# Hybrid decoder layer: the gated recurrence in two lanes of two heads, with half-width score products for the long levels

## The chip, the cores and the metric

The kernel runs on one core of a Trainium2 chip. The metric is the device time of one execution in microseconds (us); before the change the median of three runs is 2064.65 us (2059.46 to 2064.86).

## The reference

The input is a sequence of 1024 tokens of width 1024; 16 learned meta tokens go in front. One layer is computed: a half-weighted SwiGLU feed-forward network, a mixer, and a second half-weighted SwiGLU network, each behind an RMS norm. The mixer projects its input once and runs two groups of heads side by side. The change concerns the four heads of the gated recurrence (HGRN2), which works on blocks of 128 tokens:

```python
bcum = cumsum(logf)                     # per block of 128 tokens, per key channel
o_inter = (q * exp(bcum)) @ S           # what came from earlier blocks
attn[t, s] = sum_d q[t,d] * k[s,d] * exp(bcum[t,d] - bcum[s,d])   for s <= t
o = o_inter + attn @ v
S = exp(b_last)[:, None] * S + (k * exp(b_last - bcum)).T @ v
```

Each head's output is RMS-normed and gated. The other group is stick-breaking attention. Then `h = h + concat(o_recurrence, o_stickbreaking) @ w_out`.

## The kernel before

The layer is a chain of stages: first feed-forward network, projection, attention of the stick-breaking heads (with the projections of the recurrence filled in between), the recurrence, the output product, second feed-forward network. TensorE's instructions run in the order in which the program writes them; those of the other engines are placed by the tile scheduler. Every engine works its own queue in order.

**The recurrence** (`hgrn_attend`, one generator per head, each `yield` one piece of work). A head holds queries `QA`, keys `KB` and gates `F` with the 128 key channels on the partitions and the tokens along the row, and values `vT`. The decay inside a block of 128 tokens is built up in levels of n = 1, 2, 4, 8, 16, 32 and 64 tokens. At level n, blocks of 2n tokens are halved: queries of the later half meet keys of the earlier half. `level` (L870) makes the whole 128 x 128 products of all queries and all keys for the eight blocks of a head (tile `lvl`, L855, eight products, in two PSUM banks of four), and takes out of them only the pairs that belong to this level: for n up to 8 VectorE copies under a mask (L886), from n = 16 on ScalarE copies rectangles (L877). Then VectorE multiplies the later queries by the gate product of the earlier half (L904), the earlier keys by that of the later half (L908), and forms the next level's gate products `Ts` (L914). So the next level's score products wait for this level's two multiplications, which wait for this level's products. One product in float32 is two passes of TensorE, which the trace counts as two instructions. Ahead of the levels comes a diagonal (L864); behind them the keys are transposed (`km`, `knp`, L920 to L928), the block states `S` are made (`s`, `up`, L934 to L944), the output is formed (`op`, L954 and L957), normed (L962 to L967), transposed back (`onp`, L973) and split into high and low part for the output product (`oH`, L975 to L981).

**The fill.** Half of the output product, that of the stick-breaking heads, does not need the recurrence. It is 64 steps of three products with 512 columns (`wo<-...oT`, L1267), in groups of four steps for each of 16 tiles; each group reads a tile `oT` from memory, ends in an addition on VectorE (`res`, L1663) and a store (`hmN`). Its weights come from `w_out` (`mix_weights`, `split_w`): a load into `raw` (L140, two buffers), a cast into a high half `wh` on ScalarE (L145), a difference `wl` on VectorE (L147). Sixteen such weight tiles are loaded while the recurrence runs: eight for the fill, eight for the second half of the output product (`wo<-...oH`), which starts when all heads are done.

**The order.** `weave` (L1306) takes turns between the lanes and the fill by a clock: each piece yields an estimate of its TensorE time and a delay until its lane may go on. A lane that may go on comes first. The fill is held back while its spent share is ahead of the lanes' done work (`total`, `work`). Before the change there are three lanes: heads 0 and 3 one after the other, head 1, head 2. The tiles of a head exist three times; head 3 takes over the buffers of head 0. PSUM has eight banks here: two for the fill, two `z` for scores, two `tr` for transposes and states, two `o` for outputs.

Of the kernel before, what the change touches and what calls it, by code (L numbers as in the profile page):

```python
# [11 lines left out]
F32 = mybir.dt.float32  # L12
# [8 lines left out]
P = 128  # L21
# [3 lines left out]
META = 16  # L25
# [14 lines left out]
class Block:  # L40
# [784 lines left out]
    def hgrn_attend(self, h, pool, src, oH):  # L825
        nc = self.nc
# [8 lines left out]
        at8 = tile_of("attn", SEQ).rearrange("p (c t) -> p c t", t=P)  # L835
# [5 lines left out]
        ss, sq = tile_of("ss", 8), tile_of("sq", P)  # L841
        yield 0, 4000

        ps = self.flip(vT, [(0, META)])
        nc.vector.tensor_copy(vm, ps[:META, 0, :])
        for q in range(2):
            ps = self.flip(vT, [(META + (4 * q + j) * P, P) for j in range(4)])
            nc.scalar.copy(vr[:, 4 * q : 4 * q + 4, :], ps)
# [16 lines left out]

        def later(x, n):

            return x.rearrange("p (b h r) -> p b h r", h=2, r=n)[:, :, 1, :]

        def level(i, n):  # L870
            nb = P // (2 * n)
            m = later(self.masks[:, i, :], n).unsqueeze(1).broadcast_to([P, 4, nb, n])
            for half in range(2):
                ps = scores(half)
                if n >= 16:
                    for s in range(0, P, 2 * n):
                        nc.scalar.copy(  # L877
                            attn[half][s : s + n, :, s + n : s + 2 * n],
                            ps[s : s + n, :, s + n : s + 2 * n],
                        )  # L880
                    continue
                out, src = (
                    x.rearrange("p c (b h r) -> p c b h r", h=2, r=n)[:, :, :, 1, :]
                    for x in (attn[half], ps)
                )
                nc.vector.copy_predicated(out, m, src)  # L886

        diagonal()
        nc.vector.tensor_mul(QA, QA, F[:, META:])
# [1 line left out]
        tn = F  # L891
        at = 0
        for i, n in enumerate(LEVELS):
            level(i, n)
            if n <= 8:
                kb = KB.rearrange("p (b h r) -> p b h r", h=2, r=n)
                tk = tn[:, : T // n].rearrange("p (b h) -> p b h", h=2)
            else:
                kb = KB[:, META:].rearrange("p (b h r) -> p b h r", h=2, r=n)
                tk = tn[:, 1 : 1 + SEQ // n].rearrange("p (b h) -> p b h", h=2)  # L900
            nb = kb.shape[1]
            qa = QA.rearrange("p (b h r) -> p b h r", h=2, r=n)
            nq = qa.shape[1]
            nc.vector.tensor_mul(  # L904
                qa[:, :, 1, :], qa[:, :, 1, :],
                tk[:, nb - nq :, 0:1].broadcast_to([P, nq, n]),
            )
            nc.vector.tensor_mul(  # L908
                kb[:, :, 0, :], kb[:, :, 0, :], tk[:, :, 1:2].broadcast_to([P, nb, n])
            )  # L910
            o = 0 if n <= 8 else 1
            nt = Ts[:, at : at + nb + o]
            at += nb + o
            nc.vector.tensor_mul(nt[:, o : o + nb], tk[:, :, 0], tk[:, :, 1])  # L914
            tn = nt
            yield 1740, 2600
        dec = tn

        km = self.ptr.tile([P, P], F32, tag="tr", name="km")
        nc.tensor.transpose(km[:META, :], KB[:, :META], self.ident)  # L920
        nc.vector.tensor_copy(kms, km[:META, :])
        kn = vT[:, :SEQ].rearrange("p (c d) -> p c d", d=P)
# [7 lines left out]
        nc.sync.dma_start(g, src["g"][h])  # L930
        yield 960, 2000
        S = F[:, :SEQ].rearrange("p (c d) -> p c d", d=P)
        ps = self.ptr.tile([P, P], F32, tag="tr", name="s0")
        nc.tensor.matmul(ps, kms, vm, start=True, stop=True)  # L934
        nc.vector.tensor_copy(S[:, 0, :], ps)
        for q in range(2):
            ps = self.ptr.tile([P, 4, P], F32, tag="tr", name="up")
            js = [j for j in range(4) if 4 * q + j < 7]
# [413 lines left out]
    def run(self):  # L1352
# [20 lines left out]
        with ExitStack() as c0:  # L1373
# [258 lines left out]
            with tc.manual_schedule(engines={nc.tensor.engine}):  # L1632
                right, cx, pre = ExitStack(), ExitStack(), ExitStack()
                with ExitStack() as c1:
# [41 lines left out]
                    with ExitStack() as c2:  # L1676
# [3 lines left out]
                        self.pz = self.pool("pz2", 2, PSUM, c2)  # L1680
                        self.ptr = self.pool("ptr2", 2, PSUM, c2)
                        self.po = self.pool("po2", 2, PSUM, c2)
                        lanes = [chain(heads[0], heads[3]), heads[1], heads[2]]
                        self.weave(first_half_of_o(), lanes, 64 * 680.0 + 5000.0, 4 * 21900.0)

                    def begin(i, b):
                        if b not in h:
# [165 lines left out]
```

## Time and profile before

| | us |
|---|---|
| profiled execution, its time | 2062.77 |
| its span in the trace | 2061.0 |
| median of three runs | 2064.65 |
| first recurrence product to first `oH` product | 1212.67 to 1368.40 |

The span's 1.77 us less than the time lies around the program. In the table of groups each row has a line, engine, operation and tile, the count, the busy time and mean of one, and the idle time before it with what ended it. Timeline rows begin with the start in us and the duration; rows of the same kind that follow closely are merged, with their count behind `x`. A TensorE row's duration has the pipeline's end in it, so the cost of a row in a dense stretch is read from the start of one to the start of the next.

### The profile page before, as it was taken

To read this page: it belongs to the slowest core of one execution; us is meant where nothing else is said; L and a number is where in the kernel's file an instruction comes from. 1 tells how busy PE (TensorE), PEld (TensorE's weight loads), DVE (VectorE), ACT (ScalarE), POOL (GpSimd) and SP (SyncE) were. 2 spreads that over 40 slices of the span, in tenths; PEclk is the share of its full clock that TensorE was granted. 3 is DMA by queue.
4 is the path that set the end of the run, shared out by engine and by line. 5 is a ranking of instruction groups with operands and counts; after the bars stand their busy time and mean duration, and the time that the engine had idled before them with its cause. 6 is when DMAs were issued, how large, how long until landed. Compare 5 with 4: busy or idle time off the path is not lost.

```text
span 2061.0 us, 31571 instructions
## 1 busy us (share of the span) xinstructions
PE 2004.8 (97%) x11249; PEld 1782.3 (86%) x11249; DVE 1376.6 (67%) x2069; ACT 901.2 (44%) x1855; POOL 638.6 (31%) x696
## 2 busy tenths in 40 slices
PE   7999999999999999999999999999999999999999
PEld 7999999999987899988887878888888888878887
DVE  6867745556688842257878757648677677666774
ACT  7633332334554534456666623336333333234443
POOL 2366644542000002243443300210564454441000
PEclk9999999999999999999999999999999999999999
DMA  8643322227875645435454262684343333349573
GB/s 237 192 145 113 112 79 94 99 76 232 285 219 171 226 135 169 147 123 130 116 144 114 64 223 88 195 272 137 112 131 105 95 110 102 97 150 346 185 229 113
DMA packets 289647, 314.96 MB, mean 153 GB/s; under 512 B 24080, under 2 KB 218000, under 8 KB 289488
## 3 DMA queue, kind: packets, MB, share of 16 engines
q1 hardware_dynamic: 272304, 260.83, 41.1%
q0 software_dynamic: 16144, 52.10, 6.6%
q8 instruction: 89, 1.46, 0.3%
q14 instruction: 70, 0.57, 0.1%
q10 hardware_dynamic: 1040, 0.00, 0.0%
HBM read 228.62 MB, written 84.23 MB: 152 GB/s over the span
## 4 chain that ended last, share of the span: by engine, by line
PE 83%; DVE 7%; DMA 3%; ACT 3%; issue 2%; POOL 0%; SPq 0%; DVEq 0%; POOLq 0%; ACTq 0%
PE o L599 16%; PE qb L313 15%; PE qa L313 10%; PE qc L313 10%; PE proj L162 5%; PE proj L160 5%; PE proj L161 5%; PE qd L313 4%; PE o L561 3%; PE wo L1267 3%; PE flip L1086 2%; DVE wl L270 1%; PE lvl L855 1%; DVE keep L1232 1%; PE oacc L1156 1%
## 5 line engine op out<-in xcount | busy, mean ns | idle before, releaser
L313 PE MATMUL qb<-T,wh 128*128 128x384 f32 (+1 forms) x1056 | 317.8, 362 | 0.0
L270 DVE TENSOR_TENSOR wl<-s,wh 128x512 fp32r<-128x512 f32 x176 | 198.8, 1130 | 95.2 <-ACT wh L268 91.1
L313 PEld LDWEIGHTS qb<-T,wh 128*128 128x128 f32 x1056 | 195.8, 188 | 21.5
L313 PE MATMUL qa<-B,wh 128*128 128x384 f32 (+1 forms) x704 | 213.9, 367 | 0.3 <-ACT sg L415 0.3
L599 PE MATMUL o<-wl,th 128*128 128x512 f32 x539 | 209.9, 391 | 3.7 <-DVE wl L520 3.7
L599 PE MATMUL o<-wh,tl 128*128 128x512 f32 x539 | 209.6, 390 | 0.7 <-DVE tl L520 0.7
L599 PE MATMUL o<-wh,th 128*128 128x512 f32 x539 | 209.9, 391 | 0.0
L268 ACT CAST wh<-s 128x512 fp32r<-128x512 f32 x176 | 109.4, 621 | 223.2 <-PE qb L313 164.1
L160 PE MATMUL proj<-xh,wh 128*128 128x384 f32 (+2 forms) x576 | 205.0, 356 | 0.2 <-ACT xh L250 0.2
L270 DVE TENSOR_TENSOR wl<-raw,wh 128x512 fp32r<-128x512 f32 x184 | 170.1, 926 | 52.2 <-ACT wh L268 48.7
L161 PE MATMUL proj<-xh,wl 128*128 128x384 f32 (+2 forms) x576 | 199.1, 346 | 0.0
L162 PE MATMUL proj<-xl,wh 128*128 128x384 f32 (+2 forms) x576 | 198.9, 345 | 0.1
L268 ACT CAST wh<-raw 128x512 fp32r<-128x512 f32 x184 | 113.6, 620 | 184.1 <-PE qc L313 100.4
L313 PE MATMUL qb<-T,wl 128*128 128x384 f32 (+1 forms) x528 | 192.0, 364 | 0.9 <-DVE wl L270 0.9
L518 ACT CAST th<-act 128x512 fp32r<-128x512 f32 (+2 forms) x176 | 96.6, 550 | 178.1 <-PE o L599 120.0
L520 DVE TENSOR_TENSOR tl<-act,th 128x512 fp32r<-128x512 f32 (+2 forms) x176 | 105.5, 602 | 64.9 <-ACT th L518 63.7
L313 PE MATMUL qd<-X,wh 128*128 128x272 f32 x704 | 144.4, 292 | 2.0 <-DVE sp L397 1.6
L283 POOL TENSOR_TENSOR s<-raw 128x512 f32<-128x512 f32 x88 | 122.6, 1393 | 74.8 <-DVE wl L270 60.1
L313 PEld LDWEIGHTS qa<-B,wh 128*128 128x128 f32 x704 | 130.5, 188 | 16.5 <-ACT sg L415 0.7
L1232 DVE TENSOR_TENSOR_SCAN keep<-keep 128x144 f32<-128x144 f32 (+6 forms) x112 | 127.1, 1138 | 8.3 <-ACT keep L1228 6.0
L1237 POOL TENSOR_TENSOR sig<-sig,keep 128x144 f32<-128x144 f32 (+3 forms) x64 | 88.2, 1378 | 141.7 <-DVE keep L1232 75.6
L313 PE MATMUL qa<-B,wl 128*128 128x384 f32 (+1 forms) x352 | 128.8, 366 | 0.8 <-DVE wl L270 0.8
(343 smaller groups left out, 4761.1 us busy)
## 6 DMA issues: line engine op xcount, KB each, us to landing
raw<-in_ffn_w_in_dram SPq DMA_DIRECT2D x228, 256.0 KB, 3.0
raw<-in_ffn_w_out_dram SPq DMA_DIRECT2D x176, 256.0 KB, 4.3
raw<-in_w_in_dram SPq DMA_DIRECT2D x28, 512.0 KB, 4.5
ks<-kD SPq DMA_DIRECT2D x32, 260.0 KB, 5.6
oT<-oD SPq DMA_DIRECT2D x32, 256.0 KB, 4.7
ak<-in_ffn_w_out_dram SPq DMA_DIRECT2D x22, 256.0 KB, 5.3
v<-vD SPq DMA_DIRECT2D x8, 576.0 KB, 4.8
vD<-vhl SPq DMA_DIRECT2D x8, 512.0 KB, 3.9
```

Of the source, the lines that this page charges most:

```text
L160: nc.tensor.matmul(ps, wh[:, s], xs, start=k == 0, stop=False)
L161: nc.tensor.matmul(ps, wl[:, s], xs, start=False, stop=False)
L162: nc.tensor.matmul(ps, wh[:, s], xl[:, k, c0 : c0 + n], start=False, stop=k == nk - 1)
L268: nc.scalar.copy(hi, src)
L270: nc.vector.tensor_sub(lo, src, hi.bitcast(F32))
L283: op(t, x, y)
L313: nc.tensor.matmul(ps, a[:, k, :], b[:, k0 + k, :], start=start and k == 0 and i == 0, stop=k == 3 and i == 2, skip_group_check=True,)
L518: nc.scalar.copy(hi, src)
L520: nc.vector.tensor_sub(lo, src, hi.bitcast(F32))
L599: nc.tensor.matmul(banks[bank][m], z[:, m * P : (m + 1) * P], y, start=start and q == 0 and e == 0, stop=q == nq - 1 and e == 2, skip_grou ...
L1232: nc.vector.tensor_tensor_scan(out=kv, data0=kv, data1=kv, initial=1.0 if last else keep[:, end : end + 1], op0=ALU.mult, op1=ALU.bypass,)
L1237: nc.gpsimd.tensor_mul(sig, sig, keep[:, 1 : nk + 1])
```

## The change

Six edits, all in the recurrence and its weaving:

1. Levels of n = 4 and more multiply only the later halves of the queries: the moving operand has 64 columns in place of 128, read as runs of n with gaps of n. The keys stay whole as the stationary operand. All eight blocks of a head fit in one bank, so a level holds one bank in place of two. Levels 1 and 2 and the diagonal stay as they were.
2. The copies out of PSUM for these levels cover all eight blocks at once: one masked copy of 128 x 512 in place of two of 128 x 256 (n = 4, 8), and half as many rectangles, twice as long (n = 16, 32, 64).
3. `level` returns its copies, and they are issued behind the two multiplications of the level in place of ahead of them.
4. The transposed meta values (`vmp`), the keys' meta rows (`km`) and the first state (`s0`) take a bank of `o` in place of `tr`; two small copies go from VectorE to ScalarE.
5. The yield of a level of n = 4 and more says 960 ns in place of 1740.
6. Two lanes, heads 0 and 2 and heads 1 and 3, in place of three; the work estimate for the fill's share is 4 * 18000 in place of 4 * 21900.

```diff
-        ps = self.flip(vT, [(0, META)])
-        nc.vector.tensor_copy(vm, ps[:META, 0, :])
+        ps = self.po.tile([P, P], F32, tag="o", name="vmp")
+        nc.tensor.transpose(ps[:META, :], vT[:, :META], self.ident)
+        nc.scalar.copy(vm, ps[:META, :])
...
         def level(i, n):
...
-            for half in range(2):
-                ps = scores(half)
-                if n >= 16:
-                    for s in range(0, P, 2 * n):
-                        nc.scalar.copy(
-                            attn[half][s : s + n, :, s + n : s + 2 * n],
-                            ps[s : s + n, :, s + n : s + 2 * n],
-                        )
-                    continue
...
+            if n < 4:
+                m = m.unsqueeze(1).broadcast_to([P, 4, nb, n])
+                return [
+                    (later(attn[half], n), m, later(scores(half), n)) for half in range(2)
+                ]
+            ps = self.pz.tile([P, 8, P // 2], F32, tag="z", name="lvl")
+            for c in range(8):
+                nc.tensor.matmul(
+                    ps[:, c, :].rearrange("p (b r) -> p b r", r=n),
+                    KB[:, META + c * P : META + (c + 1) * P],
+                    later(QA[:, c * P : (c + 1) * P], n), start=True, stop=True,
+                )
+            if n < 16:
+                m = m.unsqueeze(1).broadcast_to([P, 8, nb, n])
+                return [(later(at8, n), m, ps.rearrange("p c (b r) -> p c b r", r=n))]
+            return [
+                (at8[s : s + n, :, s + n : s + 2 * n], None, ps[s : s + n, :, s // 2 : s // 2 + n])
+                for s in range(0, P, 2 * n)
+            ]
...
-            level(i, n)
+            copies = level(i, n)
...
+            for out, m, got in copies:
+                if m is None:
+                    nc.scalar.copy(out, got)
+                else:
+                    nc.vector.copy_predicated(out, m, got)
...
-            yield 1740, 2600
+            yield 960 if n >= 4 else 1740, 2600
...
-        km = self.ptr.tile([P, P], F32, tag="tr", name="km")
+        km = self.po.tile([P, P], F32, tag="o", name="km")
...
-        ps = self.ptr.tile([P, P], F32, tag="tr", name="s0")
+        ps = self.po.tile([P, P], F32, tag="o", name="s0")
         nc.tensor.matmul(ps, kms, vm, start=True, stop=True)
-        nc.vector.tensor_copy(S[:, 0, :], ps)
+        nc.scalar.copy(S[:, 0, :], ps)
...
-                        lanes = [chain(heads[0], heads[3]), heads[1], heads[2]]
-                        self.weave(first_half_of_o(), lanes, 64 * 680.0 + 5000.0, 4 * 21900.0)
+                        lanes = [chain(heads[0], heads[2]), chain(heads[1], heads[3])]
+                        self.weave(first_half_of_o(), lanes, 64 * 680.0 + 5000.0, 4 * 18000.0)
```

The number of TensorE passes is the same on both sides. Where they stand is not. On TensorE at the start of the recurrence (`flip`: transposes of the values, 128x64: the half-width products), before:

```order
L855 MATMUL lvl<-QA,KB 128x128 x16
L1086 MATMUL flip<-ident,vT 16x128
L1086 MATMUL flip<-ident,vT 128x128 x8
L855 MATMUL lvl<-QA,KB 128x128 x168
L920 MATMUL km<-ident,KB 16x128
```

and now:

```order
L856 MATMUL lvl<-QA,KB 128x128 x32
L1281 MATMUL wo<-wh,oT 128x512
L1281 MATMUL wo<-wl,oT 128x512
L1281 MATMUL wo<-wh,oT 128x512 x2
L1281 MATMUL wo<-wl,oT 128x512
L1281 MATMUL wo<-wh,oT 128x512
L856 MATMUL lvl<-QA,KB 128x128 x16
L1281 MATMUL wo<-wh,oT 128x512
```

Before, three heads went through nearly all levels with no fill between; now two do, and six fill products stand between the levels 1 and 2, six more behind level 2, and then by turns three and six between the half-width products of one head and the other. The second pair of heads is woven with nine fill products at a time.

On VectorE at the same place (`wl`: the low halves of the fill's weights, `Ts`: gate products; `128x128x2` is the masked copy of level 2), where the first weight half stood behind the work of several levels before:

```order
L914 TENSOR_TENSOR Ts<-Ts 128x130
L914 TENSOR_TENSOR Ts<-Ts 128x32
L147 TENSOR_TENSOR wl<-raw,wh 128x512
L904 TENSOR_TENSOR QA<-QA,Ts 128x32x16
L908 TENSOR_TENSOR KB<-KB,Ts 128x32x16
```

and now:

```order
L147 TENSOR_TENSOR wl<-raw,wh 128x512
L928 TENSOR_TENSOR Ts<-Ts 128x32
L928 TENSOR_TENSOR Ts<-Ts 128x16
L147 TENSOR_TENSOR wl<-raw,wh 128x512
L928 TENSOR_TENSOR Ts<-Ts 128x8
L147 TENSOR_TENSOR wl<-raw,wh 128x512 x2
L924 COPY_PREDICATED attn<-masks,lvl 128x128x2
L913 TENSOR_TENSOR QA<-QA,Ts 128x256x2
```

The first weight half stood at level 16 (`128x32x16` is its multiplication) and now stands ahead of the copies of level 2, with all four halves of the fill's first column block in a row.

At the end of the recurrence on TensorE, before, the last head's output products and transposes:

```order
L957 MATMUL op<-vr,attn 128x128
L1267 MATMUL wo<-wh,oT 128x512
L1267 MATMUL wo<-wl,oT 128x512
L1267 MATMUL wo<-wh,oT 128x512 x2
L1267 MATMUL wo<-wl,oT 128x512
L1267 MATMUL wo<-wh,oT 128x512 x2
```

and now:

```order
L968 MATMUL op<-F,QA 128x128
L971 MATMUL op<-vr,attn 128x128
L987 MATMUL onp<-ident,vT 128x128 x8
L1281 MATMUL wo<-wh,oH_13950 128x512
L1281 MATMUL wo<-wl,oH_13950 128x512
```

Fifteen fill products stood behind the last `op` and nine behind the last `onp`; now no fill is left there, and the last transposes follow the last output products directly.

More of the change, by code (lines that the diff above doesn't have):

```diff
@@ L866, in later @@
         def later(x, n):
+            if len(x.shape) == 3:
+                return x.rearrange("p c (b h r) -> p c b h r", h=2, r=n)[:, :, :, 1, :]
             return x.rearrange("p (b h r) -> p b h r", h=2, r=n)[:, :, 1, :]
@@ L871, in level @@
             nb = P // (2 * n)
-            m = later(self.masks[:, i, :], n).unsqueeze(1).broadcast_to([P, 4, nb, n])
-            for half in range(2):
-                ps = scores(half)
-                if n >= 16:
-                    for s in range(0, P, 2 * n):
-                        nc.scalar.copy(
-                            attn[half][s : s + n, :, s + n : s + 2 * n],
-                            ps[s : s + n, :, s + n : s + 2 * n],
-                        )
-                    continue
-                out, src = (
-                    x.rearrange("p c (b h r) -> p c b h r", h=2, r=n)[:, :, :, 1, :]
-                    for x in (attn[half], ps)
-                )
-                nc.vector.copy_predicated(out, m, src)
+            m = later(self.masks[:, i, :], n)
+            if n < 4:
[9 more added lines that the diff above has]
+                    later(QA[:, c * P : (c + 1) * P], n), start=True, stop=True,
+                )
+            if n < 16:
[5 more added lines that the diff above has]
+            ]
         diagonal()
```

## The prediction

> **What bounds the kernel now.** I read the head of the page, then the busy time by stage of the recurrence and what follows it, then the groups in it, then its timeline.
>
> ```profile
> PE 2004.8 (97%) x11249; PEld 1782.3 (86%) x11249; DVE 1376.6 (67%) x2069; ACT 901.2 (44%) x1855; POOL 638.6 (31%) x696
> ```
> ```profile
> core 0: us, PE busy (x) PEld busy (x) DVE busy (x) ACT busy (x) POOL busy (x), PEclk, DMA share, GB/s
> 1212.60:1270.00 57.40, 51.70 (x416) 47.10 (x413) 52.09 (x104) 19.46 (x58) 0.00 (x0) 1.00 0.42 141
> 1270.00:1368.40 98.40, 92.10 (x588) 80.09 (x587) 56.75 (x115) 31.36 (x111) 16.84 (x22) 1.00 0.67 213
> 1368.40:1418.50 50.10, 49.47 (x242) 41.08 (x242) 32.61 (x49) 22.99 (x47) 7.08 (x10) 1.00 0.57 195
> ```
>
> TensorE is busy for 97% of the whole, so a gain must come from less TensorE work or from fewer gaps in it. The first of the three stretches is the levels of three heads without fill: VectorE is busy 52.09 of 57.40 us there and is as near its limit as TensorE. In the second, the fill is woven in and VectorE has slack (56.75 of 98.40). The third is the second half of the output product; it starts when all heads are done, and the change does not touch it. So the prediction is about one number: when that half starts. Before, the recurrence runs from 1212.67 to 1368.40, that is 155.7 us.
>
> ```profile
> 1212.67 1.70 PE L1086 MATMUL flip<-ident,vT 128*16 128x128 f32 x10
> ```
> ```profile
> L1267 PEld LDWEIGHTS wo<-wh,oH x128: 186/188/190, 1368.4 to 1418.1; 128*128 128x128 f32 x128
> ```
>
> How much of it is TensorE work? The groups give the counts, dense stretches of the timeline the prices.
>
> ```profile
> L855 PE MATMUL lvl<-QA,KB 128*128 128x128 f32 x512 | 63.7, 279 | 4.3 <-DVE attn L886 2.5 <-ACT attn L877 1.3 <-DVE attn L864 0.2
> L1267 PE MATMUL wo<-wh,oT 128*128 128x512 f32 x128 | 44.6, 407 | 1.0 <-DMA oT<-oD 1.0
> L1267 PE MATMUL wo<-wl,oT 128*128 128x512 f32 x64 | 25.2, 394 | 0.0
> L954 PE MATMUL op<-F,QA 128*128 128x128 f32 x64 | 12.4, 276 | 0.8 <-ACT sq L962 0.8
> L957 PE MATMUL op<-vr,attn 128*128 128x128 f32 x64 | 12.4, 275 | 0.0
> L941 PE MATMUL up<-vr,vT 128*128 128x128 f32 x56 | 7.6, 284 | 0.5 <-DVE F L935 0.4
> L1086 PE MATMUL flip<-ident,vT 128*128 128x128 f32 (+1 forms) x36 | 5.4, 279 | 2.1 <-DVE vm L845 1.1 <-ACT vr L848 0.9
> L927 PE MATMUL knp<-ident,KB 128*128 128x128 f32 x32 | 4.8, 281 | 1.6 <-ACT vT L928 1.2 <-DVE kms L921 0.4
> L973 PE MATMUL onp<-ident,vT 128*128 128x128 f32 x32 | 4.2, 273 | 0.0
> ```
> ```profile
> 1303.04 0.39 PE L954 MATMUL op<-F,QA 128*128 128x128 f32 x2
> ...
> 1304.83 1.95 PE L855 MATMUL lvl<-QA,KB 128*128 128x128 f32 x16
> ...
> 1308.02 1.08 PE L973 MATMUL onp<-ident,vT 128*128 128x128 f32 x8
> 1308.85 0.48 PE L1267 MATMUL wo<-wh,oT 128*128 128x512 f32 x1
> ...
> 1324.05 1.95 PE L855 MATMUL lvl<-QA,KB 128*128 128x128 f32 x16
> 1325.75 0.48 PE L1267 MATMUL wo<-wh,oT 128*128 128x512 f32 x1
> 1326.06 0.39 PE L1267 MATMUL wo<-wl,oT 128*128 128x512 f32 x1
> ...
> 1328.63 0.49 PE L855 MATMUL lvl<-QA,KB 128*128 128x128 f32 x3
> ```
>
> From start to start: 16 score passes take 1325.75 - 1324.05 = 1.70 us, .106 each; twelve fill products 2.88, .24 each (the first costs .31, .08 more than the later .23); the 16 passes of `op` 1.79, .112 each; eight transposes .83, .104 each. Work: 512 x .106 = 54.4, 192 x .24 = 46.1, 128 x .112 = 14.3, 56 x .112 = 6.3, 100 x .104 = 10.4, sum 131.5 us. The other 24.2 us are waits (with a few small passes, on both sides alike). Until the first fill product at 1270, 368 score passes and 45 transposes were done, 43.7 us of work in 57.3: 13.6 us of waits there, 10.6 in the rest.
>
> **The change, part by part.**
>
> *Half-width products.* 20 groups of 16 passes (five levels, four heads) move 64 columns in place of 128. What such a pass costs, no row shows directly. The nearest is the small product of the first norm, also float32 with 128 columns of weights, which moves one column:
>
> ```profile
> L173 PE MATMUL nps<-ones_d,nacc x6: 163/214/250, 570.0 to 570.4; 128*128 128x1 f32 x4, 128*16 128x1 f32 x2
> ```
> ```profile
> 569.96 0.19 PEld L173 LDWEIGHTS nps<-ones_d,nacc 128*128 128x128 f32 x1
> ...
> 570.07 0.19 PEld L173 LDWEIGHTS nps<-ones_d,nacc 128*128 128x128 f32 x1
> ...
> 570.18 0.19 PEld L173 LDWEIGHTS nps<-ones_d,nacc 128*128 128x128 f32 x1
> ```
>
> The first row gives the shape, the others the start of three weight loads in a row. They follow each other at .11 us, as the score passes do, though almost nothing is moved. So a float32 pass with fresh weights of 128 columns costs .11 whatever it moves, and the keys are still loaded whole. I take no gain: 320 x 0. The other end is a pass in which the moved columns set the pace; the nearest row is the attention's output, of another number format, 128 columns in .06:
>
> ```profile
> 1198.36 0.23 PE L1156 MATMUL oacc<-wu,v 128*128 128x128 f32 x1
> 1198.42 0.22 PE L1158 MATMUL oacc<-wu,v 128*64 128x128 f32 x1
> ```
>
> By that, 320 x (.106 - .055) = 16.3 us of work would go. Above zero: the columns are now read with gaps, which no row shows; I hold a loss for unlikely, since the moved columns would have to cost twice what they do. The Trainium skill ("TensorE: Matmul & The Clock Gate", Back-to-back issue gap) gives the gap of a lone matmul by the columns moved, 134 cycles for 128 and about 60 for 64, by which the passes would halve; the same page (LDWEIGHTS) sets the load by the weight's columns, P / 1.2 ns, 107 ns for 128. The first rule would give the sum with 16.3 us off, the second the sum with nothing off, and the .11 us of the row with one moved column agree with the second.
>
> *More turns between scores and fill.* The fill stands in 30 groups in place of 18; 12 x .08 = 1.0 us.
>
> *Copies.* On VectorE 16 masked copies of 256 become 8 of 512.
>
> ```profile
> L886 DVE COPY_PREDICATED attn<-masks,lvl 128x256 f32<-128x256 uint8 x32 | 17.7, 577 | 4.4 <-PE lvl L855 4.0
> L904 DVE TENSOR_TENSOR QA<-QA,Ts 128x512 f32<-128x512 f32 x24 | 16.6, 691 | 4.2 <-PE lvl L855 4.2
> L908 DVE TENSOR_TENSOR KB<-KB,Ts 128x520 f32<-128x520 f32 (+1 forms) x24 | 16.4, 685 | 0.0
> ```
>
> One of 512 costs between .58 and 1.15. A level of two heads at n = 4 and 8 then needs 2 x (.69 + .69) + 2 x (.58 to 1.15) = 3.9 to 5.1 us of VectorE, against 2 x 1.70 + 9 x .24 = 5.6 us of TensorE: covered. The copies leave the chain from level to level (1.2 us per head and level), but the fill and the other head now stand in that time; nothing is gained on TensorE, and 1.2 us a level is lost where fill runs out. The small copies moved to ScalarE (31.36 busy of 98.40) cost nothing.
>
> *The start.* VectorE's queue decides, by the order of the changed program. From its first diagonal (1216.7 as before) to the second weight half are 30 instructions, at the first stretch's mean of 52.09 / 104 = .50: 15 us, about 1231. Then come halves 3 and 4, whose raw tiles may be loaded only when halves 1 and 2 have freed the two buffers. SyncE waits with that load at the head of its queue; the loads of `res` and `oT` stand behind it, and are wanted only later.
>
> ```profile
> 1222.80 1.26 ACT L145 CAST wh<-raw 128x512 fp32r<-128x512 f32 x2 [0.83 <-DMA raw<-in_w_out_dram]
> ```
> ```profile
> 1214.86 1.53 SPq L140 DMA_DIRECT2D raw<-in_w_out_dram  x2
> ```
> ```profile
> raw<-in_w_out_dram SPq DMA_DIRECT2D x16, 256.0 KB, 3.8
> ```
>
> Half 1 is done near 1230: + 3.8 landing + .6 cast + .7 = 1235.1, half 4 at 1235.7. VectorE stands still for 3.5 us with the masked copies of level 2 behind it, and TensorE for want of free banks. Copy .6, scores .85, copy chain, scores .85, six fill products 1.4: level 4 starts at 1240.2. By then 18 transposes, 96 passes and 12 products are done, 15.0 us in 27.5: 12.5 us of waits. From there to level 64 TensorE is the longer side, with no wait.
>
> *Between the pairs.* Transposes, states and outputs of heads 0 and 1 meet on two `tr` and two `o` banks, as before. I take 3.8 us (state updates .5, an output half that waits for the norm of the one before it in its bank 1.2, `onp` and `flip` in one pair of banks 2.1), between 0 and 6.
>
> *The second pair.* Head 3's values load behind one more raw tile; some 9 us of fill and scores lie ahead of their use. But weight half 12 stands in VectorE's queue ahead of head 3's diagonal, and its raw tile waits for half 10: about 2 us, between 0 and 5.
>
> *The end.* Before, fifteen fill products hid the norm of the last output.
>
> ```profile
> 1360.85 0.48 PE L1267 MATMUL wo<-wh,oT 128*128 128x512 f32 x1
> ...
> 1365.71 1.04 PE L973 MATMUL onp<-ident,vT 128*128 128x128 f32 x8
> ```
> ```profile
> 1363.28 0.69 DVE L967 TENSOR_TENSOR vT<-op,ss 128x512 f32<-128x512 f32 x1
> ```
>
> From the end of the last `op` pass, where the fill goes on, to the normed half is 1363.97 - 1360.85 = 3.1 us. No fill is left there now, so this is bare, with 1 us for the other head's squares ahead on ScalarE, 1 for weight half 15 in VectorE's queue and .5 for the `o` bank: 5.5, between 3 and 7.
>
> *The sum.* Waits, small passes (1.3) and turns after: 12.5 + 3.8 + 2.0 + 5.5 + 1.3 + 1.0 = 26.1 against 24.2: + 1.9 us. On the profiled execution, 2062.77 + 1.9 = 2064.7; on the median of the runs, 1.9 above it, 2066.5. I say 2065. The bounds of the parts added the favourable way (between the pairs - 3.8, second pair - 2, end - 2.5) give - 6.4, the other way (+ 2.2, + 3, + 1.5) + 8.6: 2058 to 2073 for this case by itself. A measurement can tell about .3% from no change, 6.2 us: within 2058.5 to 2070.8 counts as the same.
>
> **The rivals.** *Half columns, half price.* The rows of `oacc` speak for it, the one-column product against. Work - 16.3; TensorE then needs 3.9 us a level, as much as VectorE, and on the four pairs of levels 4 and 8 up to 1.2 us each of waits comes back, say 4 in all: 1.9 - 16.3 + 4 = - 10.4, 2052. The Trainium skill's table of issue gaps, named above, would have it so; by its rule on the load it would not. Chance .17.
>
> *VectorE blocked behind the weights* (slower). Three times (halves 3, 12 and 15) a weight half that waits for its load stands ahead of work that a lane needs. I took 3.8 us of landing. The first two raw tiles needed 1222.80 - 1214.86 = 7.9 us. Each us over 3.8 counts three times; from 1.4 on (5.2 us of landing) the kernel is slower by more than .3%, and at 6.5 it is 2.7 x 3 = 8 later: 2073. For it speaks the full DMA of the last stretch, against it that raw tiles landed in 3.8 in the median. Chance .22.
>
> *The fill covers more than I see:* the joints between the pairs and of the second pair vanish, the rest as forecast: 1.9 - 3.8 - 2.0 = - 3.9, 2059. Chance .11; half of it under the bound.
>
> **How the numbers follow.** The forecast (no gain of work, waits traded for waits) has .5. Faster by over .3%: .17 and half of .11, .22. Slower: .2 of the second rival, and .04 of the forecast's own upper end, .24. Within: .54. The range takes in the first rival's time and most of the second's: 2052 to 2073; half of each, some .2, lies outside.
>
> **What would show it.** In the changed profile: half-width passes at .11 from start to start (at .06 the first rival holds); VectorE idle near 1231 until a cast of `wh`, and level 4 starting near 1240; a wait of 3 us or more ahead of the last `onp`; the first `oH` product at 1370, within 6. Wrong would be a first `oH` product before 1362, or waits that sum to far less than 24.

## The result, and the profile after

The changed kernel takes 2068.41 us (median of 22 executions, 2063.58 to 2071.78), the kernel before 2064.65 beside it. The ratio is 1.002, with a 95% interval of 1.0012 to 1.0027: slower by 2.5 to 5.6 us. That is within 0.3%, and inside the range. The profiled execution took 2068.88 us, its span is 2067.2. In it the recurrence runs from 1214.31 to 1374.52, 160.2 us. For the kernel before, 1368.40 is the weight load ahead of the first `oH` product; the product itself starts at 1368.68, so from product to product it is 156.0 us there, not 155.7, and the stretch is 4.2 us longer now. Everything ahead of it is the same program and stands 1.64 us later here, which is taken off where times are compared with the forecast.

The stretches of the profile after, the two long ones of before first, then short ones at both ends (PEclk is the third column from the right):

```profile
1212.60:1270.00 57.40, 50.09 (x338) 44.80 (x337) 41.74 (x79) 12.51 (x29) 2.20 (x4) 0.94 0.67 227
1270.00:1368.40 98.40, 93.67 (x655) 83.00 (x654) 64.84 (x124) 32.20 (x106) 12.06 (x16) 1.00 0.57 183
1225.00:1230.00 5.00, 1.60 (x9) 1.15 (x9) 4.97 (x13) 0.71 (x2) 0.00 (x0) 1.00 0.33 99
1230.00:1235.00 5.00, 3.79 (x13) 3.31 (x13) 2.46 (x10) 0.62 (x1) 0.00 (x0) 0.55 0.48 134
1235.00:1240.00 5.00, 4.08 (x25) 3.62 (x25) 4.17 (x7) 0.62 (x1) 0.00 (x0) 0.77 0.95 287
1370.00:1375.00 5.00, 1.83 (x9) 1.65 (x10) 2.86 (x7) 2.17 (x10) 2.85 (x2) 0.88 0.34 109
1375.00:1380.00 5.00, 5.00 (x18) 3.92 (x17) 1.34 (x2) 0.62 (x1) 1.28 (x1) 0.78 0.75 214
```

VectorE is busy 41.74 us in the first stretch, where it had 52.09. But the granted clock, 1.00 in all three stretches of the profile before, is 0.94 in the first stretch: behind five us in which TensorE worked only 1.60, it fell to half, and at the end again. No part of the forecast had that.

What a half-width pass costs is read from its tile (its weight loads, the wide masked copy) and from a dense place of TensorE's timeline:

```profile
L884 PEld LDWEIGHTS lvl<-QA,KB x320: 186/192/192, 1241.4 to 1351.8; 128*128 128x128 f32 x160
...
L924 DVE COPY_PREDICATED attn<-masks,lvl x24: 695/718/779, 1222.8 to 1335.1; 128x256 f32<-128x256 uint8 x16, 128x512 f32<-128x512 uint8 x8
```
```profile
1231.21 0.80 PE L1281 MATMUL wo<-wl,oT 128*128 128x512 f32 x1 [3.96 <-DVE wl L147]
...
1233.51 4.87 PE L856 MATMUL lvl<-QA,KB 128*128 128x128 f32 x24
...
1241.61 1.89 PE L884 MATMUL lvl<-QA,KB 128*128 128x64 f32 x16
1243.32 0.48 PE L1281 MATMUL wo<-wh,oT 128*128 128x512 f32 x1
```

Sixteen half-width passes take 1243.32 - 1241.61 = 1.71 us, .107 each: nothing was saved. The same rows show the start. TensorE stands 3.96 us ahead of the first product with `wl`; then 24 whole score passes last 4.87 us, .2 each, the half clock. On VectorE at that time:

```profile
1230.47 0.68 DVE L147 TENSOR_TENSOR wl<-raw,wh 128x512 fp32r<-128x512 f32 x1
...
1231.38 0.68 DVE L147 TENSOR_TENSOR wl<-raw,wh 128x512 fp32r<-128x512 f32 x1
...
1234.65 0.69 DVE L147 TENSOR_TENSOR wl<-raw,wh 128x512 fp32r<-128x512 f32 x1 [2.50 <-ACT wh L145]
1235.80 0.69 DVE L147 TENSOR_TENSOR wl<-raw,wh 128x512 fp32r<-128x512 f32 x1 [0.46 <-ACT wh L145]
1236.41 0.71 DVE L924 COPY_PREDICATED attn<-masks,lvl 128x256 f32<-128x256 uint8 x1
```

The two waits for a cast stand where they were forecast, with the masked copy of level 2 behind them. And the end is bare, as forecast: three groups of transposes, each behind a norm.

```profile
1367.30 0.66 PE L987 MATMUL onp<-ident,vT 128*128 128x128 f32 x4 [0.66 <-DVE vT L981]
...
1371.42 0.63 PE L987 MATMUL onp<-ident,vT 128*128 128x128 f32 x4 [1.68 <-DVE vT L981]
1373.80 1.07 PE L987 MATMUL onp<-ident,vT 128*128 128x128 f32 x4 [1.75 <-DVE vT L981]
1374.52 0.77 PE L1281 MATMUL wo<-wh,oH 128*128 128x512 f32 x1
```

### The profile page after: what moved, and what is told of

It reads as the page before. It is cut to its first block, busy times and chain, and to the rows that moved or that the text cites. A ratio compares the mean times of both kernels' runs of the same rounds, so it can differ in the third digit from the quotient of the medians.

```text
span 2067.2 us, 31521 instructions
## 1 busy us (share of the span) xinstructions
PE 2007.4 (97%) x11249; PEld 1786.1 (86%) x11249; DVE 1372.5 (66%) x2053; ACT 897.7 (43%) x1835; POOL 638.8 (31%) x696
## 4 chain that ended last, share of the span: by engine, by line
PE 86%; DVE 7%; ACT 3%; issue 2%; DMA 1%; POOL 0%; SPq 0%; DVEq 0%; ACTq 0%; POOLq 0%
PE o L599 17%; PE qb L313 15%; PE qa L313 10%; PE qc L313 10%; PE proj L162 5%; PE proj L160 5%; PE proj L161 5%; PE wo L1281 4%; PE qd L313 4%; PE o L561 3%; PE flip L1100 2%; PE lvl L884 2%; DVE wl L270 2%; DVE keep L1246 1%; PE oacc L1170 1%
```

## The experiments

Each kernel was timed in five rounds against the kernel before on the same chip. The times of the kernel before differ by some us between these series (2061.68 beside the first four runs, 2063.88 beside the next four, 2064.77 beside the last four), so the ratio decides. The two runs with 64 columns of weights in all long levels leave out half of these levels' scores; they answer a question and are no candidates.

| what | us | ratio to before (95%) |
|---|---|---|
| the change | 2068.41 | 1.0020 (1.0012 to 1.0027) |
| edits 1 to 5 in three lanes | 2080.53 | 1.0068 (1.0040 to 1.0096) |
| two lanes alone | 2065.45 | 1.0017 (1.0009 to 1.0026) |
| four raw buffers | 2067.76 | 1.0024 (1.0015 to 1.0034) |
| 64 columns of weights | 2054.50 | 0.9961 (0.9948 to 0.9974) |
| fill starts behind level 2 | 2062.84 | 1.0000 (0.9988 to 1.0012) |
| fill starts later still | 2074.16 | 1.0048 (1.0035 to 1.0061) |
| fill kept for the end | 2069.29 | 1.0022 (1.0013 to 1.0030) |
| three lanes, whole products | 2073.98 | 1.0046 (1.0033 to 1.0059) |
| fill later still, 64 columns of weights | 2052.08 | 0.9939 (0.9926 to 0.9952) |
| `wl` on GpSimd | 2065.63 | 1.0012 (1.0002 to 1.0023) |
| combination | 2058.49 | 0.9970 (0.9959 to 0.9981) |
| combination, `wl` on GpSimd | 2064.71 | 0.9998 (0.9988 to 1.0007) |

### Which edit costs: two lanes alone

Edit 6 made on the kernel before:

```diff
-lanes = [chain(heads[0], heads[3]), heads[1], heads[2]]
-self.weave(first_half_of_o(), lanes, 64 * 680.0 + 5000.0, 4 * 21900.0)
+lanes = [chain(heads[0], heads[2]), chain(heads[1], heads[3])]
+self.weave(first_half_of_o(), lanes, 64 * 680.0 + 5000.0, 4 * 18000.0)
```

> The kernel before with only edit 6 made: two lanes and the share 4 * 18000, whole products in two banks, copies ahead of the multiplications. Theory A (waits of two lanes): the fill starts early, the weight halves stand in VectorE's queue as in the changed kernel and the last onp is bare, 2066 to 2076 us. Theory B (products, copies, banks): like before, 2061 to 2066 us.

In us the result lies inside B's span and just under A's, but those spans were set from a kernel before at 2064.65, and it ran at 2061.68 here. By the ratio the lanes alone cost 1.9 to 5.4 us, about as much as the whole change. The wait at the start is that of the changed kernel, the clock falls behind it as well (0.50 from 1230 to 1235 us), and 1.76 us of wait stand ahead of the last `onp`:

```profile
1231.00 0.79 PE L1267 MATMUL wo<-wl,oT 128*128 128x512 f32 x1 [4.03 <-DVE wl L147]
```

So A's waits hold: two lanes are enough for a loss of this size. That the other edits cost nothing doesn't follow; the next run speaks against it.

### Which edit costs: the other five in three lanes

Edit 6 undone on the changed kernel:

```diff
-lanes = [chain(heads[0], heads[2]), chain(heads[1], heads[3])]
-self.weave(first_half_of_o(), lanes, 64 * 680.0 + 5000.0, 4 * 18000.0)
+lanes = [chain(heads[0], heads[3]), heads[1], heads[2]]
+self.weave(first_half_of_o(), lanes, 64 * 680.0 + 5000.0, 4 * 21900.0)
```

> The changed kernel with only edit 6 undone: three lanes and the share 4 * 21900, with half-width products, wide copies behind the multiplications and the other banks kept. Theory A (a half-width pass costs the .107 us of a full one; the loss lies in the waits that two lanes bring, about 4 us at the start where weight halves 3 and 4 wait for the two raw buffers, 5 at the bare end): the start is as before the change and fill hides the last norm, so 2058 to 2066 us and no wait over 1 us ahead of the last onp. Theory B (the products, copies or banks cost the time themselves, the lanes nothing): 2067 us or more.

A missed, with its time and with its mark: a wait of 1.82 us stands ahead of the last `onp`. B's number (2067 or more) came, for the most part by the clock. The nine executions fall in two groups: three of 2065.05 to 2065.45 with a mean clock of .997 or .998 over the whole execution, six of 2079.01 to 2088.46 with .986 to .990. The profiled one is of the second group:

```profile
1245.00:1260.00 15.00, 12.91 (x99) 12.10 (x97) 12.12 (x21) 2.26 (x6) 0.00 (x0) 0.95 0.12 36
1260.00:1275.00 15.00, 14.18 (x61) 13.41 (x61) 6.48 (x11) 3.10 (x9) 0.00 (x0) 0.50 0.06 19
1275.00:1290.00 15.00, 15.00 (x69) 14.71 (x69) 4.75 (x8) 2.35 (x7) 0.57 (x1) 0.50 0.21 70
```

For 30 us TensorE has hardly a gap (29.18 of 30 us busy) and runs at half its clock. The busy share hides this; only PEclk and the count show it (61 and 69 instructions where the row ahead has 99). It raised the question whether half-width products themselves keep the clock down, theory C below. By the ratio the five edits cost 8 to 20 us in three lanes, the lanes alone 2 to 5, and both together 2.5 to 5.6: the costs don't add up, so the loss can't be put down to one side alone.

### What a half-width pass costs: 64 columns of weights

```diff
-    ps[:, c, :].rearrange("p (b r) -> p b r", r=n),
-    KB[:, META + c * P : META + (c + 1) * P],
+    ps[:64, c, :].rearrange("p (b r) -> p b r", r=n),
+    KB[:, META + c * P : META + c * P + 64],
...
```

> The changed kernel with 64 columns of weights in place of 128 in every half-width product: only the first 64 keys of a block meet the later queries, so half of the scores of these levels are left out and the copies take what stands in the first 64 rows. As many passes, as many moved columns. Theory A (loading 128 columns of weights sets the .107 us of a half-width pass): passes from start to start at .05 to .06, 16 us of TensorE work less, of which up to 6 come back as waits: 2052 to 2058 us. Rival (a fixed cost of each pass, or the moved columns read with gaps, sets the pace): passes stay at .107 and the time at 2067 to 2070.

Rows of its tile and of a dense place:

```profile
L884 PEld LDWEIGHTS lvl<-QA,KB x320: 132/138/138, 1240.7 to 1338.6; 128*64 128x64 f32 x160
```
```profile
1250.01 1.15 PE L884 MATMUL lvl<-QA,KB 128*64 128x64 f32 x16
1251.09 0.50 PE L1281 MATMUL wo<-wh,oT 128*128 128x512 f32 x1
```

With as many moved columns and half the weights, sixteen passes take 1.08 us, .067 each. 320 x (.107 - .067) = 12.8 us; by the ratios the kernel is 2064 x (1.0020 - .9961) = 12.2 faster than the changed one. So the 128 columns of weights pace the half-width pass. The pass was expected at .05 to .06 and is a little dearer, the direction and the time are as expected. The Trainium skill ("TensorE: Matmul & The Clock Gate", LDWEIGHTS (loading the stationary operand)) sets a load at P / 1.2 ns, 53 ns for 64 columns and 107 for 128: the second agrees with the .107 here, the first is below the .067.

### The start: four raw buffers

The raw tiles get a pool of their own with four buffers while the recurrence runs.

```diff
-raw = self.wp.tile([P, n], F32, tag="raw", name="raw", bufs=self.raw_bufs)
+wp, bufs = self.raw_pool or (self.wp, self.raw_bufs)
+raw = wp.tile([P, n], F32, tag="raw", name="raw", bufs=bufs)
...
+self.raw_pool = self.pool("rawp", ctx=c2), 4
```

> The changed kernel with four raw buffers in place of two while the recurrence runs; the order on TensorE is the same to the last instruction. Theory A (VectorE stands still near 1231 us because halves 3 and 4 wait for the raw buffers of 1 and 2, and TensorE's clock falls after its 4 us of waiting): the wait of 3.96 us ahead of the third wl product goes, the granted clock from 1212 to 1245 us stays at 1.00, and the time falls by 4 to 6 us, 2062 to 2065. Rival (the start is bound by VectorE's work or by the two z banks, the weights only happen to be late): 2067 to 2070, with the wait in another place.

The waits for a cast are gone from VectorE, four `wl` stand in one row, and the time is the same:

```profile
1226.81 1.79 DVE L929 TENSOR_TENSOR Ts<-Ts 128x65 f32<-128x65 f32 x10
1228.52 2.49 DVE L148 TENSOR_TENSOR wl<-raw,wh 128x512 fp32r<-128x512 f32 x4
1233.51 0.73 DVE L925 COPY_PREDICATED attn<-masks,lvl 128x256 f32<-128x256 uint8 x1 [2.49 <-PE lvl L857]
```
```profile
1229.27 0.79 PE L1282 MATMUL wo<-wl,oT 128*128 128x512 f32 x1 [4.07 <-DVE wl L148]
...
1231.57 4.32 PE L857 MATMUL lvl<-QA,KB 128*128 128x128 f32 x24
```

VectorE now waits 2.49 us for TensorE, which stood 4.07 us ahead of its first `wl` product and then went through 24 passes at half clock. Theory A falls for the raw buffers: two waits stood side by side, and taking one away leaves the other. The one that stays is the order: the first fill products stand ahead of the second head's level 2, VectorE makes ten `Ts` and the multiplications before the first `wl`, and TensorE cannot pass.

### The start: the fill behind level 2

```diff
-yield 5000.0
+yield 12000.0
...
-self.weave(first_half_of_o(), lanes, 64 * 680.0 + 5000.0, 4 * 18000.0)
+self.weave(first_half_of_o(), lanes, 64 * 680.0 + 12000.0, 4 * 18000.0)
```

> The changed kernel with a fill that starts later in TensorE's written order: its first step counts 12000 in place of 5000, so the first six fill products stand behind level 2 of both heads, and nine fill products more are left for the end. Theory A2 (the wait at the start is TensorE's own order: the first product with wl stands about 5 us ahead of its weights and blocks the score products behind it; the halved clock follows from that wait): that wait falls below 2 us, the granted clock from 1225 to 1245 us rises to 0.9 or more, and the time falls by 3 to 6 us, 2062 to 2066. Rival (VectorE is full until 1230 us and sets the start by itself): the wait only changes its name, level 4 starts as late, 2066 to 2070.

The wait of 4 us is gone, level 4 starts 20.1 us behind the first product in place of 27.3 (with six fill products, 1.4 us, fewer ahead of it), and by the ratios the kernel is about 4 us faster than the changed one. The start isn't all of it: more fill is left for the end, where one wait of 2.98 us stands ahead of the last `onp` in place of .66, 1.68 and 1.75. Of A2's marks, the clock came only in part:

```profile
1230.00:1235.00 5.00, 3.81 (x28) 3.60 (x28) 4.92 (x10) 0.00 (x0) 0.00 (x0) 1.00 0.35 102
1235.00:1240.00 5.00, 3.50 (x15) 2.86 (x15) 3.50 (x8) 1.24 (x2) 0.00 (x0) 0.69 0.98 278
```

It falls later, at a smaller wait (1.27 us for `wl`, ended at 1237.44), and not in every execution: over the twelve, the time goes from 2057.14 us at a mean clock of 1.000 to 2071.05 at .994, between these two 2.3 us for each thousandth.

### The clock: the fill later still

```diff
-yield 5000.0
+yield 18000.0
...
-self.weave(first_half_of_o(), lanes, 64 * 680.0 + 5000.0, 4 * 18000.0)
+self.weave(first_half_of_o(), lanes, 64 * 680.0 + 18000.0, 4 * 18000.0)
```

> The changed kernel with the first fill step counted at 18000 in place of 5000: 72 products of the levels 1 to 16 stand ahead of the first fill product, and only three fill products stand between two levels of the first pair after that; 21 fill products are left for the end. Theory C (TensorE's clock is granted by how many columns move, so a stretch of half-width products with little fill runs at half speed even when TensorE hardly waits): a stretch of 10 us or more between 1240 and 1280 us has a granted clock near 0.5, and the time is 2072 to 2090. Rival (the clock falls only behind a wait of TensorE of 3 us or more): the clock stays at 1.00, the bare end is covered, 2060 to 2066.

As theory C expected, in place and in time:

```profile
1236.19 5.07 PE L884 MATMUL lvl<-QA,KB 128*128 128x64 f32 x32 [0.66 <-DVE attn L924]
...
1245.71 0.77 PE L1281 MATMUL wo<-wh,oT 128*128 128x512 f32 x1
...
1247.14 3.51 PE L884 MATMUL lvl<-QA,KB 128*128 128x64 f32 x16
1250.40 0.77 PE L1281 MATMUL wo<-wh,oT 128*128 128x512 f32 x1
```
```profile
1240.00:1245.00 5.00, 5.00 (x22) 4.71 (x22) 3.21 (x6) 0.00 (x0) 0.00 (x0) 0.50 0.09 21
...
1255.00:1260.00 5.00, 5.00 (x23) 4.71 (x22) 2.08 (x4) 1.64 (x5) 0.57 (x1) 0.50 0.41 125
```

TensorE is busy without a gap for 20 us and stays at half speed (16 passes take 1250.40 - 1247.14 = 3.26 us, .204 each). The clock falls in the course of the 32 passes from 1236.19 on, behind a wait of .66 us; in the ten us ahead of them no wait is over 1.39. So the rival, which asks for a wait of 3 us, falls. The Trainium skill ("TensorE: Matmul & The Clock Gate", Part 1: The HAM clock gate) has the clock at half after an idle window of about 3.4 us and at full after a busy one. The fall in the changed kernel, behind a wait of 3.96 us, agrees, and so does it that the clock is either half or full; the fall here does not, and neither does the return, if busy means a full busy column. The measurement decides.

### The clock: whole products in three lanes

The five edits in three lanes, but every level with the whole products of levels 1 and 2, in two banks and with copies of half the size; so edits 1 and 2 are undone, and 3 to 5 are left:

```diff
-ps = self.pz.tile([P, 8, P // 2], F32, tag="z", name="lvl")
...
+pss = [scores(half) for half in range(2)]
+return [(later(attn[half], n), m, later(pss[half], n)) for half in range(2)]
```

> Three lanes with the edits 2 to 5 but whole products: the same order on TensorE as in the run with three lanes and half-width products, each level again in two banks with copies of half the size, behind the multiplications. Theory C (half-width products lower the granted clock, since fewer columns move in the same time): the granted clock is 1.00 throughout although there are at least as many waits, no execution lies above 2070, and the profiled one is 2058 to 2068. Rival (many waits of 0.5 to 2 us in the levels lower the clock): it falls to 0.5 for 10 us or more as with half-width products, and some executions lie above 2075.

The time is 2074, beyond what C allowed, but not for the clock: it falls in short stretches and comes back within five us, in the middle of score passes alone.

```profile
1226.13 3.60 PE L856 MATMUL lvl<-QA,KB 128*128 128x128 f32 x16 [1.02 <-DVE attn L916]
```
```profile
1225.00:1230.00 5.00, 3.71 (x17) 3.34 (x16) 4.22 (x9) 0.24 (x1) 0.00 (x0) 0.66 1.12 333
1230.00:1235.00 5.00, 3.07 (x24) 2.83 (x24) 4.56 (x9) 0.00 (x0) 0.00 (x0) 1.00 0.05 14
```

The rest are waits: TensorE works 3.07 to 4.4 us of five in the levels, and waits for VectorE's copies (L916). That the copies, now behind the multiplications, hold two banks longer is the likely reason; edits 3 to 5 were not tried one by one. By the ratio these three edits cost 7 to 12 us in three lanes, without any half-width product. So waits make the clock fall, with whole products too, and C is right in one half: whole products bring it back, half-width ones do not.

### The clock: the fill later still, 64 columns of weights

The edits of the late fill and of the 64 columns of weights together.

> The late fill (first step 18000), on which the clock fell for 24 us, now with 64 columns of weights in every half-width product; only the first 64 keys of a block meet the later queries, so half of these levels' scores are left out. Order on TensorE and moved columns as in the late fill. A half-width pass at half speed then moves 64 columns in about .107 us, 600 per us, as a whole pass does at half speed (128 in .213), and not 300. Theory C (the clock comes back only when more than some 300 columns move per us): the granted clock is back at 1.00 within 8 us of its fall, against 24, and the time is 2045 to 2056 us. Rival (the narrow reads with gaps themselves hold it down, or the waits, of which there are more now): it stays near 0.5 for 12 us or more, 2058 to 2068.

```profile
1235.00:1240.00 5.00, 5.00 (x38) 3.96 (x38) 5.00 (x9) 0.00 (x0) 0.00 (x0) 0.66 0.44 136
1240.00:1245.00 5.00, 4.74 (x47) 3.43 (x46) 4.01 (x9) 2.80 (x10) 0.00 (x0) 1.00 0.34 108
```

The same narrow reads in the same order, loaded with fewer weights, move their columns in less time, and the clock is back within five us. The time is as expected, and the rival falls. But that the columns moved per us decide, as C has it, does not agree with the rows. In the late fill, three fill products and the first half of a level's passes, 3 x 512 + 8 x 64 = 2048 columns, take 3.06 us from 1245.71 on, 669 per us, and the clock stays down. Sixteen whole passes are 2048 columns too; from 1226.13 on, in the run before this one, they take 3.60 us, 569 per us, and the clock comes back at their end. What fits all three runs is the share of the time in which columns move: a half-width pass with 128 columns of weights takes .107 us for columns that need no more than .067 with 64. No run tested this by itself, and the bound is open.

### The end: fill kept for it

```diff
-self.weave(first_half_of_o(), lanes, 64 * 680.0 + 5000.0, 4 * 18000.0)
+self.weave(first_half_of_o(), lanes, 64 * 680.0 + 5000.0, 4 * 20000.0)
```

> The changed kernel with the fill's share at 4 * 20000 in place of 4 * 18000: the start is the same, less fill stands behind the state products and in the second pair's levels, and 15 fill products stand ahead of, and six behind, the last onp. Theory A (the bare end costs 4 to 5 us, and 1 us more by the clock that falls there): the waits ahead of the last two onp groups go below 1 us, the clock at the end stays at 1.00, and the time falls by 3 to 5 us, 2063 to 2066. Rival (the fill is missed where it is taken away): as many waits between the pairs and in the second pair as were saved at the end, 2067 to 2070.

No wait is left ahead of the last `onp` groups, and the time stays, so A's time fails. A wait has taken their place, but not where the rival said; it stands 7 us behind the first `oH` product:

```profile
1382.40 0.50 PE L1281 MATMUL wo<-wh,oH 128*128 128x512 f32 x1 [3.46 <-ACT wh L145]
```
```profile
1370.09 0.33 SPq L140 DMA_DIRECT2D raw<-in_w_out_dram  x1
1370.52 5.65 SPq L275 DMA_DIRECT2D raw<-in_ffn_w_in_dram  x6
1376.26 0.64 SPq L140 DMA_DIRECT2D raw<-in_w_out_dram  x1
```

The last raw tile of the output product came to stand behind six loads of the next stage on SyncE's queue, and its half is cast 10 us after the fill's end. In the changed kernel the last two raw loads start at 1361.94, ahead of those six. That fill which ends later frees the weight buffers later is the likely reason.

### The weights on GpSimd

For the 16 weight tiles of the output product only:

```diff
-nc.vector.tensor_sub(lo, raw, hi.bitcast(F32))
+(nc.gpsimd if self.low_on_pool else nc.vector).tensor_sub(lo, raw, hi.bitcast(F32))
```

> The changed kernel with the low halves wl of the output product's 16 weight tiles made by GpSimd in place of VectorE; the order on TensorE is the same. Theory D (the waits at the start and at the end come from the place of the weight halves in VectorE's queue, behind ten Ts and ahead of the copies, the last norm's products and so on): the wait of 4 us ahead of the first wl product falls below 2 us, the granted clock from 1225 to 1245 us is 0.9 or more, the wait ahead of the last onp falls by a us or more, and the time by 4 to 7 us, 2061 to 2065. Rival (a difference of 128x512 takes GpSimd some 1.5 us where VectorE needs .6, as its row for oH says, and four of them stand in a row; or GpSimd slows VectorE): the wait stays over 3 us, 2067 to 2072.

By the ratios 1.7 us faster than the changed kernel, less than half of what D said, and the two intervals overlap. The wait for `wl` is gone, but the clock falls as before (.52 from 1235 to 1240 us), the wait ahead of the last `onp` is 1.74 us, and a wait for VectorE itself stands in place of that for `wl`:

```profile
1234.09 3.90 PE L856 MATMUL lvl<-QA,KB 128*128 128x128 f32 x16 [3.86 <-DVE attn L924]
```
```profile
1225.70 1.40 DVE L928 TENSOR_TENSOR Ts<-Ts 128x260 f32<-128x260 f32 x1
...
1230.56 2.85 DVE L928 TENSOR_TENSOR Ts<-Ts 128x65 f32<-128x65 f32 x10
```

The masked copy comes behind the same `Ts`, and beside GpSimd they are slower (2.85 us for ten that took 1.79 above). That GpSimd slows VectorE and that a wait of over 3 us stays is the rival's; its time is not.

### A version that beats both

```diff
-self.weights("wo", 2, 8, c1)
+self.weights("wo", 3, 8, c1)
...
-yield 5000.0
+yield 12000.0
...
-self.weave(first_half_of_o(), lanes, 64 * 680.0 + 5000.0, 4 * 18000.0)
+self.weave(first_half_of_o(), lanes, 64 * 680.0 + 12000.0, 4 * 19500.0)
...
+w = P if n < 64 else 64
-    ps[:, c, :].rearrange("p (b r) -> p b r", r=n),
-    KB[:, META + c * P : META + (c + 1) * P],
+    ps[:w, c, :].rearrange("p (b r) -> p b r", r=n), KB[:, k0 : k0 + w],
```

> A combination: the fill starts behind level 2 (first step 12000), its share is 4 * 19500 so that six fill products stand ahead of the last onp, level 64 loads only the 64 keys of the earlier half as weights (all that the level needs, nothing is left out), and three raw buffers. Sum of the parts: 2068.4 less 4.5 for the start, less 4 heads x 16 passes x .053 = 3.4 for level 64, less 3 at the end = 2057.5 us, 2054 to 2062; faster than both kernels. Rival (what the fill covers at the end comes back behind it, since the last weight halves take the buffers that the last fill products free): a wait of 3 us or more within 12 us of the first oH product, 2061 to 2066.

2058.49 us, by the ratio's interval 3.9 to 8.5 less than before. That is the time summed, though not each part: at the .067 measured above, level 64 saves 64 x .04 = 2.6 us (an estimate) and not 3.4. At the start there is no wait for `wl` and no fall of the clock:

```profile
1235.00:1240.00 5.00, 5.00 (x41) 4.64 (x39) 5.00 (x12) 0.37 (x1) 0.00 (x0) 1.00 0.94 292
```

With the order mended, the third raw buffer seems to matter after all: the halves that the fill behind level 2 waited for (1.27 us) are in time here. That was not tried by itself. At the end 2.92 us of wait are left ahead of the last `onp`. Level 64 is the only level whose earlier keys lie in one piece; for the others a load of 64 columns that leaves nothing out would have to gather keys, which was not tried.

The same with the low halves on GpSimd:

> The combination above, with the low halves wl on GpSimd. Theory D: VectorE's queue is free of the weights, so another 1 to 4 us less than with them on VectorE, 2052 to 2060. Rival (GpSimd's longer differences make the last halves later still): 2060 to 2068.

2064.71 us, the rival's time, but not in the way that it said. VectorE is slowed, and TensorE waits 5.32 us for a masked copy of level 2 at the start:

```profile
1233.86 3.75 PE L856 MATMUL lvl<-QA,KB 128*128 128x128 f32 x16 [5.32 <-DVE attn L925]
```

## Why the prediction was right, and where it was not

**Half-width products: right.** No gain was taken, .107 was measured, and the run with 64 columns of weights shows the cause. The first rival falls with it.

**Copies: covered, as said, but misread.** A masked copy of 512 takes .70 us, inside .58 to 1.15, and levels 4 to 64 run without a wait but one of .40. The .58 was the mean of two kinds: before, the copies of levels 1 and 2 take about .72 us, those of levels 4 and 8, the ones replaced, .43. The first row is from before, the second from after:

```profile
1245.96 0.43 DVE L886 COPY_PREDICATED attn<-masks,lvl 128x256 f32<-128x256 uint8 x1
```
```profile
1244.76 0.70 DVE L924 COPY_PREDICATED attn<-masks,lvl 128x512 f32<-128x512 uint8 x1
```

So a wide copy saves VectorE .16 us against two narrow ones (.86 less .70), and not up to .58.

**The start: right in size by luck, wrong in its cause.** Level 4 starts at 1241.61 - 1.64 = 1239.97 where 1240.2 was forecast. The step put it down to the halves 3 and 4 and their raw buffers. With four buffers nothing changes; the fill in another place gives most of the time back. The forecast step missed the other two parts of the chain: TensorE's own order ahead of the first `wl`, and the half clock behind that wait. The clock alone is some 3 us of the 12.3 us that are counted as waits below (an estimate: half of the 6.8 us at half speed, less the .5 of them that fall in the wait), and the forecast had no such term.

**Between the pairs: a little small.** Summed from start to start, the waits there are 4.5 us (forecast 3.8): 1.2 about the state products, 1.8 ahead of the second output half, 1.6 about `flip` and `onp`.

**Second pair:** 1.25 us for a forecast of 2.0. **The end:** from the last fill product on, 1374.52 - 1364.26 = 10.26 us less 5.24 of work is 5.0 for a forecast of 5.5, by the norm and the weights as said. The sign given for it, one wait of 3 us or more ahead of the last `onp`, did not come: the waits are of .66, 1.68 and 1.75 us. That the clock falls there as well was not said.

**The sum: here it failed by 2.6 us.** The start's wait is 27.3 us less 15.0 of work, 12.3; with the other three, 4.5 + 1.25 + 5.0, the named waits are 23.1 us, against 23.8 in the forecast. But the recurrence of 160.2 us less 131.5 of work leaves 28.7, so the rest (small passes, turns, gaps under .2 us, the .40 ahead of a level) is 5.6 us and not 1.3 + 1.0; the eight passes of `s` alone are 8 x .205 = 1.6. On the side of before, all of that was inside the 24.2 us that the work left over (24.5, counted to the first `oH` product); on the side of after, only named pieces were added up. The two sides were counted in different ways, and the difference went into the answer.

**The second rival** (VectorE blocked behind the weights) named a real wait, but its price per us of landing did not hold: where the waits for the load were taken away, nothing was gained. **The third** did not come: the joints are still there.

**The chances.** The likeliest case came, in its upper half. Beside the small pieces, the clock has a part in that which no term had: the changed kernel's executions have a mean clock of .996 to .998, .997 on the mean; those of before, beside the experiments, .995 to 1.000, .998 on the mean; and a thousandth of 2067 us is 2.1 us where TensorE sets the end. How much of the 4 us is clock and how much is wait was not separated, since the wait brings the clock down.

## What to carry to other kernels

Before making a float32 product narrower, look at which operand sets its pace: here the weights did, so halving the moved columns saved nothing, and halving the weights saved 12 us (in a kernel that leaves out half of these scores). Where fill is woven into an engine that works in order, its first product must not stand ahead of its weights; and read PEclk beside the busy share, for a TensorE that is busy 100% can be at half speed. When a wait is taken away, ask what stood beside it: of four repairs tried one by one, two left the time as it was, one gave 1.7 us within the noise, and only the later fill gave about 4.

## What the runs showed of the hardware

- TensorE's clock fell to half behind a stretch of five us in which it had worked 1.60, for (.45 + .23) x 5 / .5 = 6.8 us; with half-width products of 128 weight columns it fell behind a wait of no more than .66 us, and stayed at half for 20 us and more, fully busy. Whole products, or 64 weight columns, brought it back within five us.
- The masked copy of 512 takes VectorE .70 us where one of 256 of the same levels took .43: twice the columns, 1.6 times the time. On levels 1 and 2 one of 256 takes about .72, so the columns alone do not set the price.
- Beside GpSimd's differences, VectorE's small products take up to some three times as long (128x260: 1.40 us for .43), and a `wl` of .69 us took 1.80 next to the splitting of `oH`:

```profile
1368.66 1.80 DVE L147 TENSOR_TENSOR wl<-raw,wh 128x512 fp32r<-128x512 f32 x1
```
